# A hybrid decoder layer step: no paged units beside the last head, weight subtractions on GpSimd in two halves, sample rows as sums

## The chip, the cores and the metric

One core of a Trainium2 chip. The metric is the device time of one execution in microseconds (us), the median of several runs. Engines: PE (TensorE matmul; PEld is its weight load), DVE (VectorE), ACT (ScalarE), POOL (GpSimd), SP (SyncE, which issues most of the DMAs).

## What is computed

One layer for a prompt of 1024 rows with 16 meta rows ahead of it, and for 8 sample rows that each have 4096 past positions in a paged cache (32 pages of 128 positions, with keys and values of 512 columns). The model width is 1024, the input projection has 2560 columns, the attention 4 heads with two softmax maps each, the FFN 2816 hidden columns. All is float32.

```
proj = rms_norm(x, ln_mix_pre) @ w_in            # split into q, k, v, a, g
u = a * sigmoid(g)                               # conv group, 512 channels
s = einsum(q, k) * HEAD_DIM**-0.5 - slopes * dist   # causal, two maps per head
p = softmax(s)
o = einsum(p[:, :, 0] - lam * p[:, :, 1], v)
...
attn_out = rms_norm(o, subln) * (1 - lambda_init)
conv_out = silu(layer_norm(causal_depthwise(u, conv_w, conv_b)))
mix = concat([attn_out, conv_out]) @ w_out
x = x + rms_norm(mix, ln_mix_post)
h = rms_norm(x, ln_ffn_pre)
x = x + rms_norm((silu(h @ w_gate) * (h @ w_up)) @ w_down, ln_ffn_post)
```

The sample rows go through the same, with k and v of their own pages ahead of their own row.

## The kernel before

Matmuls of float32 values are made from two parts of each operand: a rounded part H and the rest L = raw - H, so three matmuls stand for one (L149 to L151). A weight row of 128x1024 is brought by `load_split` (L133 to L141): SP loads it as `raw`, ACT casts it to H, and one engine makes L by one subtraction of 128x1024. For 15 rows of `w_in` (wi0 to wi7, wi13 to wi19) and for the 8 rows of `w_out` (wo0 to wo7) this engine is POOL; for the other five of `w_in` it is DVE.

The prompt's rows come in three chunks of columns. `xchunk` (L182 to L204) transposes eight blocks of 128 channels into eight PSUM banks; for each, ACT writes xH, DVE writes xL, and, in the first chunk alone, whose first eight columns are the sample rows, DVE scales these eight columns from PSUM into `xsT`. The sample rows' own projection reads `xsT`.

The stages in time: loads and first chunks (0 to 40 us); the conv group's projections and its depthwise convolution on DVE and POOL (40 to 140 us and on); head by head the projections of q, k, v and the prompt's attention (140 to 442 us, the last head from 372 us on); eight output blocks `c_block` (w_out, residual, norm), of 48 matmuls each; the FFN's gate, up and down to the end.

The prompt's attention of head h runs over eight row blocks i (`attn`, L477 to L575): PE makes the scores in one, two or three pieces (L507), DVE adds the position bias and takes the row's minimum of the negated score (L509), ACT takes the exponentials of both maps (L515), DVE combines them to A = p0 + cc * p1 (L526, in pieces of columns 0 to 400 and the rest, where a row has more than 400), PE transposes A (L534), ACT copies it out (L538), and PE multiplies by the values (L548). After blocks 3 and 7, ACT takes row sums of squares (`junk`, L562), POOL makes their inverse root `or` (L564), ACT scales the head's output `oh` (L566) and PE transposes it (L571).

The samples' paged attention is written as a generator, `dec_units` (L751 to L787). A key unit loads two pages (`page_pair`, by SP, at most 8 page loads ahead), POOL multiplies them by the query (L680, two products of 128x512), and DVE sums the products over 64 columns (L690). With all 16 pairs of a sample done, `dec_max` has DVE make maxima and POOL reduce them over the partitions (L707); `dec_exp` subtracts that maximum on DVE (L712) and takes the exponential on ACT. A value unit loads two value pages and, once for two pairs, issues eight matmuls `pv` on PE (L732). Units are called by `dec_step(rate)`, which adds the rate to what is owed and runs the whole part of it. In the main loop, head h's row blocks call it with `rate_b[h]`, the output blocks with `rate_c`, the FFN's steps with `rate_d`. All of it stands in the order of priorities that a scheduler keeps: a unit's instructions are placed behind the prompt's by an offset, and the scheduler orders the instructions of each engine by its own estimate of when they can start. The flag `kv_n[1]` becomes true once the loop over heads and row blocks is through (L1355).

Of the kernel before, what the change touches and what calls it, by code (L numbers as in the profile page):

```python
# [8 lines left out]
F32 = mybir.dt.float32  # L9
# [3 lines left out]
ALU = mybir.AluOpType  # L13
# [7 lines left out]
DB = 8  # L21
# [25 lines left out]
def tile_layer(ctx: ExitStack, tc: tile.TileContext, I, O, cfg):  # L47
    nc = tc.nc
    V, S, G, T, D = nc.vector, nc.scalar, nc.gpsimd, nc.tensor, nc.sync
# [5 lines left out]
    at = ctx.enter_context(tc.tile_pool(name="at", bufs=cfg["at"]))  # L55
# [4 lines left out]
    def slab(name, dt=F32):  # L60
        return slp.tile([P, SLAB], dt, tag="slab", name=name)

    kv_n = [0, False]
# [66 lines left out]
    def load_raw(src, name, n3=True):  # L130
        raw = slab(name + "r")
        D.dma_start(kn(raw) if n3 else raw[:, :1024], src)
        return raw  # L133

    def load_split(src, name, l_eng, n3=True):
        raw = early.pop(name, None) or load_raw(src, name, n3)
        H = slab(name + "H", F32R)
        S.copy(H[:, :1024], raw[:, :1024])
        L = slab(name + "L", F32R)
        l_eng.tensor_tensor(L[:, :1024], raw[:, :1024], H[:, :1024].bitcast(F32), op=ALU.subtract)  # L140
        return H, L  # L141

    point = {}
# [10 lines left out]
    xH = [slab(f"xH{k}", F32R) for k in range(8)]  # L154
    xL = [slab(f"xL{k}", F32R) for k in range(8)]
# [13 lines left out]
    def xprep(b):  # L169
        rows = DB + META if b < 0 else P  # L170
        xt = x_st.pop(b)
        if "j" not in x_st:
            x_st["j"] = kv("xsq")
        ssq = smt(f"xs{b}", 1)
        S.activation(x_st["j"][:rows], xt[:rows, :DM], AF.Square, accum_out=ssq[:rows])
        r = rstd_of(ssq[:rows], rows, 1.0 / DM, f"xr{b}")
        eng = G if b in cfg["xn_g"] else V
        eng.tensor_scalar(xt[:rows, :DM], xt[:rows, :DM], r[:rows], None, op0=ALU.mult)
        return xt, rows

    xsT = cst.tile([P, 8, DB], F32, name="xsT")
# [3 lines left out]
    def xchunk(c):  # L185
        c0, w = CHUNKS[c]
        blks = [xprep(b) for b in ([-1, 0, 1], [2, 3, 4], [5, 6, 7])[c]]
        if c == 0 and cfg["wi_first"]:
            for ft in (12, 16):
                w_in_load(ft)  # L190
        pts = [f(f"xT{c}{k}") for k, f in enumerate(XPS[c])]
        off = 0
        for xn, rows in blks:
            for k, pt in enumerate(pts):
                T.transpose(out=pt[:, off : off + rows], in_=xn[:rows, k * P : (k + 1) * P], identity=ident[:rows, :rows])
            off += rows
        for k, pt in enumerate(pts):
            wk = wpre[:, k : k + 1]
            S.mul(xH[k][:, c0 : c0 + w], pt[:, :w], wk)
            V.scalar_tensor_tensor(  # L200
                xL[k][:, c0 : c0 + w], pt[:, :w], wk, xH[k][:, c0 : c0 + w].bitcast(F32), op0=ALU.mult, op1=ALU.subtract
            )
            if c == 0:
                V.tensor_scalar(xsT[:, k, :], pt[:, 0:DB], wk, None, op0=ALU.mult)  # L204

    w_in_v = I["w_in"][0].rearrange("(k p) n -> p k n", p=P)

# [6 lines left out]
    def w_in_load(ft):  # L214
        if ft not in ahead:
            ahead[ft] = load_split(w_in_src(ft), f"wi{ft}", V if ft in cfg["wi_v"] else G)
# [454 lines left out]
    def dec_scores(b, st):  # L671
        qB = dec.tile([P, 512], F32, tag="qB", name=f"qB{b}")
        D.dma_start(qB, qsD[b].partition_broadcast(P))
        s = dec.tile([P, NPG + 1, 8], F32, tag="s", name=f"s{b}", bufs=3)
        st[b] = s
        for pg in range(0, NPG, 2):
            kt = page_pair(ck, b, pg, f"k{b}_{pg}")
            n = b * NPG // 2 + pg // 2
            for i in range(2):
                x = G.tensor_tensor(kt[:, i, :], kt[:, i, :], qB, op=ALU.mult)  # L680
            products.append((s[:, pg : pg + 2, :], kt))
            if len(products) > cfg["rlag"]:
                head_sums(x)
            yield b
# [3 lines left out]
    def head_sums(after):  # L688
        s, kt = products.pop(0)
        x = V.tensor_reduce(  # L690
            s.rearrange("p a c -> p (a c)"), kt.rearrange("p a (c d) -> p (a c) d", d=HD), axis=AX.X, op=ALU.add
        )
        if after is not None:
            tc.add_manual_dep(x.ins, after.ins.name, behind, reason="sums behind a later product")

    def dec_max(b, st):
        s = st[b]
        V.tensor_tensor(
            s[:, :NPG, :].rearrange("p g (h j) -> p (g h) j", j=2),
            s[:, :NPG, :].rearrange("p g (h j) -> p (g h) j", j=2),  # L700
            dbias.rearrange("p g h -> p (g h)").unsqueeze(2).to_broadcast([P, NPG * NH, 2]), op=ALU.add,
        )
        V.tensor_copy(s[:, NPG, :], selfs[:, b, :])
        m = smt(f"dm{b}", 8, 2)
        V.tensor_reduce(m, s.rearrange("p g c -> p c g"), axis=AX.X, op=ALU.max)
        mg = smt(f"dg{b}", 8, 2)
        G.partition_all_reduce(mg, m, P, bass.bass_isa.ReduceOp.max)  # L707
        st[b] = s, mg

    def dec_exp(b, st):  # L710
        s, mg = st[b]
        V.tensor_tensor(s, s, mg.unsqueeze(1).to_broadcast([P, NPG + 1, 8]), op=ALU.subtract)  # L712
        S.activation(s, s, AF.Exp)
        st[b] = s
# [5 lines left out]
    def dec_values(b, st):  # L720
        a = st.pop(b)
        pv = pdec(f"pv{b}")
        vs = []
        for pg in range(0, NPG, 2):
            if not vs:
                size = min(cfg["vgrp"] if kv_n[1] else 2, (NPG - pg) // 2)
            vs.append((pg, page_pair(cv, b, pg, f"v{b}_{pg}")))
            if len(vs) == size:
                for q, vt in vs:
                    for i in range(2):  # L730
                        g = (q + i) % 4
                        x = T.matmul(  # L732
                            pv[32 * g : 32 * g + 8, :], lhsT=a[:, q + i, :], rhs=vt[:, i, :],
                            start=q + i < 4, stop=q + i >= NPG - 4, tile_position=(0, 32 * g),
                        )
                        if vt is not vs[-1][1]:
                            tc.add_manual_dep(x.ins, page_dmas[-1], together, reason="pages side by side")
                vs = []
            if pg == NPG // 2:
                dec_total(b, a)  # L740
            yield 0 if vs else size
        pvs = dec.tile([P, 512], F32, tag="gs", name=f"pvs{b}", bufs=2)
        for g in range(4):
            S.copy(pvs[32 * g : 32 * g + 8, :], pv[32 * g : 32 * g + 8, :])
            S.dma_start(pvD[b, g], pvs[32 * g : 32 * g + 8, :])

    def dec_units():
        st = {}
        ks = (b for bb in range(DB) for b in dec_scores(bb, st))
        nk, ready, exped, at = 0, 0, 0, []  # L750
        per = NPG // 2  # L751

        def softmaxes(all_=False):
            nonlocal ready, exped
            while "k" in nat and ready < (nk - len(products)) // per:
                dec_max(ready, st)
                at.append(nk)
                ready += 1
            while exped < ready and (all_ or nk >= at[exped] + cfg["elag"]):
                dec_exp(exped, st)  # L760
                exped += 1

        def keys(n):
            nonlocal nk
            for _ in range(n):
                if nk < DB * per:
                    next(ks)
                    nk += 1
                    if nk == DB * per:
                        while products:  # L770
                            head_sums(None)
                    softmaxes(nk == DB * per)
                    yield

        yield from keys(per + cfg["lag"])
        while "k" not in nat:
            yield "wait"
        softmaxes(True)
        for b in range(DB):
            for n in dec_values(b, st):  # L780
                yield
                yield from keys(n)
# [60 lines left out]
    def w_out_load(k):  # L843
        wo.append(load_split(I["w_out"][0, k * P : (k + 1) * P, :], f"wo{k}", G, n3=False))
# [544 lines left out]
    xn_g=(), wi_first=1, wi_e=(13, 17), sq=0,  # L1389
    behind=-400, w0=7, w1=7, wi_n=1, anchor=1, wi_v=(8, 9, 10, 11, 12), taps=11, conv=400, r2_g=1, hb=5,  # L1390
    vgrp=2, fing=5, ml_g=0, fend=22, cst=0, db=3, cn=6, scn=12, wo0=27, wor=2, c0=7,
    at=8, slabs=35, kv=4, p=6, dve_mul=0, rate_b=(1, 1.25, 1, 0.75), rate_c=1, rate_d=2.45, rate_s=2.2,
    ffn_l=lambda nc: nc.vector,
)
_INS = [
# [39 lines left out]
```

## Time and profile before

| | us |
|---|---|
| median of 3 runs | 1434.7 |
| lowest, highest | 1431.78, 1438.51 |
| the profiled execution | 1440.69 |
| its span in the trace | 1438.8 |
| PE busy | 1357.1 (94%) |
| DVE busy | 860.9 (60%) |
| POOL busy | 595.2 (41%) |
| ACT busy | 551.2 (38%) |
| mean granted clock of PE | 0.977 |

How to read it: the profile shows one execution, 6.0 us longer than the median of the runs. "Busy" is the time in which an engine has an instruction running, and a running instruction may be one that stands still. PE's share is high over the whole span, but the stages differ, and the stage from 372 to 442 us is the one with the least of it.

### The profile page before, as it was taken

The page shows a single profiled execution, that of the slowest core. Times are in us where ns is not written, and L with a number is a line of the kernel's source. Part 1 is how long each engine was busy: PE and PEld are TensorE (multiplying, and loading weights), DVE is VectorE, ACT ScalarE, POOL GpSimd, SP SyncE. Part 2 cuts the span into 40 slices and gives each one's busy share as a digit, 9 for nine tenths or more (in the row PEclk, how much of TensorE's full clock was granted, in tenths as well). Part 3 has the DMA queues.
Part 4 walks back from the last instruction along what each step waited for, and adds up shares of the span by engine and source line. Part 5 has one row for each costly group of instructions (what it writes and reads, how often), then busy time and mean ns, then how long its engine had stood idle before and what let it go on. Part 6 is the DMA issues. An engine that isn't in the chain of part 4 may idle for free.

```text
span 1438.8 us, 21552 instructions
## 1 busy us (share of the span) xinstructions
PE 1357.1 (94%) x6960; PEld 1057.1 (73%) x6960; DVE 860.9 (60%) x1403; ACT 551.2 (38%) x1112; POOL 595.2 (41%) x479
## 2 busy tenths in 40 slices
PE   5999899989869999999999989999999989999997
PEld 5999799979747787777776757676776765666666
DVE  5689996936684567566645465654653374452158
ACT  6566878797764345113021121312121112211122
POOL 4598867445372113745545455464530000000023
PEclk9999999999889999999999999999999999999999
DMA  8211015226535548678867857777677656763454
GB/s 246 86 59 38 27 55 163 75 96 192 170 98 193 171 148 269 211 259 260 262 226 235 265 199 249 235 257 264 204 263 221 214 163 218 229 190 125 147 195 172
DMA packets 199677, 264.34 MB, mean 184 GB/s; under 512 B 16423, under 2 KB 99816, under 8 KB 199557
## 3 DMA queue, kind: packets, MB, share of 16 engines
q1 hardware_dynamic: 188912, 254.40, 54.3%
q10 hardware_dynamic: 10653, 8.57, 1.8%
q8 instruction: 55, 0.90, 0.3%
q14 instruction: 57, 0.47, 0.1%
HBM read 245.92 MB, written 17.48 MB: 183 GB/s over the span
## 4 chain that ended last, share of the span: by engine, by line
PE 59%; SPq 3%; DMA 3%; issue 3%; DVE 3%; POOL 2%; ACT 1%; POOLq 0%; DVEq 0%; ACTq 0%
PE dn L149 5%; PE pu L149 5%; PE dn L150 5%; PE dn L151 5%; PE pu L151 5%; PE pu L150 5%; PE pg L149 5%; PE pg L150 5%; PE pg L151 5%; PE pv L732 4%; PE mo L151 2%; PE mo L149 2%; PE mo L150 2%; DMA v<-in_cache_v 2%; SPq L665 2%
## 5 line engine op out<-in xcount | busy, mean ns | idle before, releaser
L680 POOL TENSOR_TENSOR k<-k,qB 128x512 f32<-128x512 f32 x256 | 353.5, 1409 | 230.2 <-DMA k<-in_cache_k 176.3
L690 DVE TENSOR_REDUCE s<-k 128x16 f32<-128x1024 f32 x128 | 154.8, 1213 | 101.1 <-POOL k L680 100.9
L956 ACT CAST wH<-wr 128x1024 fp32r<-128x1024 f32 x66 | 69.0, 1048 | 239.4 <-DVE wL L958 124.6
L149 PE MATMUL dn<-wH,aH 128*128 128x512 f32 x352 | 141.3, 405 | 5.0 <-DVE y L999 3.4
L149 PE MATMUL pu<-hH,wH 128*128 128x512 f32 x352 | 141.2, 401 | 1.1 <-DVE y L999 1.1
L150 PE MATMUL dn<-wL,aH 128*128 128x512 f32 x352 | 140.9, 400 | 0.0
L151 PE MATMUL pu<-hH,wL 128*128 128x512 f32 x352 | 139.2, 396 | 1.6 <-DVE wL L958 1.6
L151 PE MATMUL dn<-wH,aL 128*128 128x512 f32 x352 | 140.7, 400 | 0.0
L149 PE MATMUL pg<-hH,wH 128*128 128x512 f32 x352 | 140.4, 399 | 0.0
L150 PE MATMUL pu<-hL,wH 128*128 128x512 f32 x352 | 140.1, 398 | 0.0
L150 PE MATMUL pg<-hL,wH 128*128 128x512 f32 x352 | 139.3, 396 | 0.0
L151 PE MATMUL pg<-hH,wL 128*128 128x512 f32 x352 | 139.2, 395 | 0.0
L958 DVE TENSOR_TENSOR wL<-wr,wH 128x1024 fp32r<-128x1024 f32 x66 | 93.7, 1420 | 46.3 <-ACT wH L956 22.2
L999 DVE TENSOR_TENSOR y<-dn,y 128x512 f32<-128x512 f32 x144 | 95.5, 684 | 38.0 <-PE dn L151 37.1
L414 POOL TENSOR_TENSOR cb<-cb 128x512 f32<-128x512 f32 x80 | 102.9, 1316 | 18.0 <-ACT cb L413 9.9
L1071 POOL TENSOR_TENSOR y<-y,wfpost 128x512 f32<-128x512 f32 x10 | 17.6, 1772 | 206.7 <-ACT ft L1069 206.6
L423 DVE SCALAR_TENSOR_TENSOR acc<-u,cw,acc 128x512 f32<-128x512 f32 x144 | 98.7, 747 | 0.2
L982 ACT CAST aH<-sg 128x512 fp32r<-128x512 f32 x44 | 27.3, 620 | 167.6 <-DVE sg L975 167.5
L149 PEld LDWEIGHTS dn<-wH,aH 128*128 128x128 f32 x352 | 67.5, 192 | 31.8 <-DVE y L999 6.8
L149 PEld LDWEIGHTS pu<-hH,wH 128*128 128x128 f32 x352 | 66.4, 189 | 29.4 <-issue 12.9
L975 DVE TENSOR_TENSOR sg<-sg,pu 128x512 f32<-128x512 f32 x44 | 30.1, 683 | 94.0 <-PE pu L151 94.0
L149 PEld LDWEIGHTS pg<-hH,wH 128*128 128x128 f32 x352 | 66.1, 188 | 27.4 <-issue 11.6
(581 smaller groups left out, 2969.5 us busy)
## 6 DMA issues: line engine op xcount, KB each, us to landing
k<-in_cache_k SPq DMA_DIRECT2D x256, 256.0 KB
v<-in_cache_v SPq DMA_DIRECT2D x256, 256.0 KB
wr<-in_w_gate SPq DMA_DIRECT2D x22, 512.0 KB
wr<-in_w_up SPq DMA_DIRECT2D x22, 512.0 KB
wr<-in_w_down SPq DMA_DIRECT2D x22, 512.0 KB
sd<-in_w_down SPq DMA_DIRECT2D x22, 512.0 KB
sw_gate<-in_w_gate SPq DMA_DIRECT2D x20, 512.0 KB
sw_up<-in_w_up SPq DMA_DIRECT2D x20, 512.0 KB
```

Of the source, the lines that this page charges most:

```text
L149: T.matmul(out, lhsT=wH, rhs=xH, start=first, stop=False)
L150: T.matmul(out, lhsT=wH, rhs=xL, start=False, stop=False)
L151: mark(T.matmul(out, lhsT=wL, rhs=xH, start=False, stop=last))
L414: G.tensor_tensor(accp, accp, t, op=ALU.add)
L423: V.scalar_tensor_tensor(dst, src, cw[:, ct, k : k + 1], acc, op0=ALU.mult, op1=ALU.add)
L680: x = G.tensor_tensor(kt[:, i, :], kt[:, i, :], qB, op=ALU.mult)
L690: x = V.tensor_reduce(s.rearrange("p a c -> p (a c)"), kt.rearrange("p a (c d) -> p (a c) d", d=HD), axis=AX.X, op=ALU.add)
L732: x = T.matmul(pv[32 * g : 32 * g + 8, :], lhsT=a[:, q + i, :], rhs=vt[:, i, :], start=q + i < 4, stop=q + i >= NPG - 4, tile_position=(0, ...
L956: S.copy(H[:, :1024], raw[:, :1024])
L958: V.tensor_tensor(L[:, :1024], raw[:, :1024], H[:, :1024].bitcast(F32), op=ALU.subtract)
L975: V.tensor_tensor(sg, sg, o, op=ALU.mult)
L999: V.tensor_tensor(y[b][:, ws], o, y[b][:, ws], op=ALU.add)
```

## The change

Four edits. `load_split` splits POOL's subtraction into two of 128x512; DVE's stay whole. `xsT` is no longer scaled from PSUM inside the loop over the eight banks, but is the sum xH + xL of the same eight columns, from SBUF, in a loop behind. The exponential of a sample's scores is allowed only once `kv_n[1]` is set, or in a call with `all_`. The rate of paged units beside head 3 goes from 0.75 to 0, and that beside the output blocks from 1 to 1.75.

```diff
         S.copy(H[:, :1024], raw[:, :1024])
         L = slab(name + "L", F32R)
-        l_eng.tensor_tensor(L[:, :1024], raw[:, :1024], H[:, :1024].bitcast(F32), op=ALU.subtract)
+        for a in (0, 512) if l_eng is G else (0,):
+            e = a + 512 if l_eng is G else 1024
+            l_eng.tensor_tensor(L[:, a:e], raw[:, a:e], H[:, a:e].bitcast(F32), op=ALU.subtract)
         return H, L
...
-            if c == 0:
-                V.tensor_scalar(xsT[:, k, :], pt[:, 0:DB], wk, None, op0=ALU.mult)
+        if c == 0:
+            for k in range(8):
+                V.tensor_tensor(xsT[:, k, :], xH[k][:, 0:DB].bitcast(F32), xL[k][:, 0:DB].bitcast(F32), op=ALU.add)
...
-            while exped < ready and (all_ or nk >= at[exped] + cfg["elag"]):
+            while exped < ready and (all_ or kv_n[1] and nk >= at[exped] + cfg["elag"]):
                 dec_exp(exped, st)
                 exped += 1
...
-    at=8, slabs=35, kv=4, p=6, dve_mul=0, rate_b=(1, 1.25, 1, 0.75), rate_c=1, rate_d=2.45, rate_s=2.2,
+    at=8, slabs=35, kv=4, p=6, dve_mul=0, rate_b=(1, 1.25, 1, 0), rate_c=1.75, rate_d=2.45, rate_s=2.2,
```

What POOL has in its order beside head 3, from wo2 on, before (wo2L to wo7L are the subtractions of `w_out`, k_12 to k_16 the products of key pages, `or` the root of a head's row sums):

```order
L140 TENSOR_TENSOR wo2L<-wo2r,wo2H 128x1024
L680 TENSOR_TENSOR k_12_4847<-k_12_4847,qB_4070 128x512
L140 TENSOR_TENSOR wo3L<-wo3r,wo3H 128x1024
L564 TENSOR_TENSOR or_4841<-ssq_3954,mhalf 128x4
L140 TENSOR_TENSOR wo4L<-wo4r,wo4H 128x1024
L140 TENSOR_TENSOR wo5L<-wo5r,wo5H 128x1024
L680 TENSOR_TENSOR k_14_5090<-k_14_5090,qB_4070 128x512 x2
L140 TENSOR_TENSOR wo6L<-wo6r,wo6H 128x1024
L680 TENSOR_TENSOR k_16_5242<-k_16_5242,qB_4070 128x512
L140 TENSOR_TENSOR wo7L<-wo7r,wo7H 128x1024
L564 TENSOR_TENSOR or_5072<-ssq_4874,mhalf 128x4
```

and after, at the same place:

```order
L142 TENSOR_TENSOR wo2L<-wo2r,wo2H 128x512 x2
L683 TENSOR_TENSOR k_12_4862<-k_12_4862,qB_4084 128x512
L142 TENSOR_TENSOR wo3L<-wo3r,wo3H 128x512 x2
L567 TENSOR_TENSOR or_4856<-ssq_3968,mhalf 128x4
L142 TENSOR_TENSOR wo4L<-wo4r,wo4H 128x512 x2
L142 TENSOR_TENSOR wo5L<-wo5r,wo5H 128x512 x2
L142 TENSOR_TENSOR wo6L<-wo6r,wo6H 128x512 x2
L142 TENSOR_TENSOR wo7L<-wo7r,wo7H 128x512 x2
L567 TENSOR_TENSOR or_5034<-ssq_4889,mhalf 128x4
```

The products of pairs 14 and 16 have left this place for the output blocks; the product of pair 12 and the roots kept theirs, and each subtraction is now two in a row.

DVE's order around the first paged exponential's subtraction (s minus dg), amid the scores and combinations of head 3, before:

```order
L526 SCALAR_TENSOR_TENSOR p_4772<-p_4785,cc_4800,p_4772 128x640
L509 ISA p_4908,nm_4902<-S_0_4909,alibi 128x272
L509 ISA nm_4902 128x1
L526 SCALAR_TENSOR_TENSOR p_4876<-p_4881,cc_4888,p_4876 128x144
L712 TENSOR_TENSOR s_2014<-s_2014,dg_4769 128x264
L509 ISA p_4965,nm_4964<-S_0_4966,alibi 128x400
```

and after:

```order
L529 SCALAR_TENSOR_TENSOR p_4787<-p_4800,cc_4815,p_4787 128x640
L512 ISA p_4923,nm_4917<-S_0_4924,alibi 128x272
L512 ISA nm_4917 128x1
L529 SCALAR_TENSOR_TENSOR p_4891<-p_4896,cc_4903,p_4891 128x144
L715 TENSOR_TENSOR s_2024<-s_2024,dg_4784 128x264
L512 ISA p_4954,nm_4953<-S_0_4955,alibi 128x400
```

Nothing moved here: the subtraction stands in the same row of DVE's order in both.

DVE's order in the first chunk of `xchunk`, the first two of the eight banks, before:

```order
L200 SCALAR_TENSOR_TENSOR xL_102<-xT_192,wpre,xH_94 128x280
L204 TENSOR_SCALAR xsT<-xT_192,wpre 128x8
L123 TENSOR_SCALAR xr_t<-xs_262 128x1
L178 TENSOR_SCALAR xt_148<-xt_148,xr_r 128x1024
L200 SCALAR_TENSOR_TENSOR xL_103<-xT_193,wpre,xH_95 128x280
L204 TENSOR_SCALAR xsT<-xT_193,wpre 128x8
```

and after:

```order
L202 SCALAR_TENSOR_TENSOR xL_102<-xT_193,wpre,xH_94 128x280
L207 TENSOR_TENSOR xsT<-xH_94,xL_102 128x8
L123 TENSOR_SCALAR xr_t<-xs_263 128x1
L202 SCALAR_TENSOR_TENSOR xL_103<-xT_194,wpre,xH_95 128x280
L180 TENSOR_SCALAR xt_148<-xt_148,xr_r 128x1024
L207 TENSOR_TENSOR xsT<-xH_95,xL_103 128x8
```

The scheduler still puts each sample sum close behind its xL, and the second xL now stands ahead of the row block's normalization `xt`.

## Rows read from the trace of the kernel before

**Rows 1.** Three stages: stretch, length, busy PE PEld DVE ACT POOL, PEclk, DMA share, GB/s.

```profile
140.00:215.00 75.00, 66.75 (x405) 63.61 (x404) 72.93 (x151) 62.19 (x141) 56.59 (x44) 0.95 0.14 41
...
372.00:442.00 70.00, 46.41 (x268) 39.69 (x267) 49.97 (x124) 44.88 (x117) 35.40 (x22) 0.78 0.47 149
442.00:700.00 258.00, 257.46 (x1202) 194.38 (x1202) 155.41 (x215) 81.10 (x165) 106.05 (x87) 1.00 0.68 221
```

**Rows 2.** PE's waits, 372 to 442 us: in total, times, longest (us).

```profile
PE S L507 <- DVE nm L509: 11.1, 6, 4.1
PE oT L571 <- ACT oh L566: 4.8, 1, 4.8
```

**Rows 3.** DVE's timeline beside head 3: start, duration, operation [idle before, releaser].

```profile
390.61 0.43 DVE L712 TENSOR_TENSOR s<-s,dg 128x264 f32<-128x264 f32 x1 [4.55 <-POOL dg L707]
...
402.27 1.22 DVE L690 TENSOR_REDUCE s<-k 128x16 f32<-128x1024 f32 x1 [4.85 <-POOL k L680]
...
403.82 2.39 DVE L526 SCALAR_TENSOR_TENSOR p<-p,cc,p 128x400 f32<-128x400 f32 x1
...
407.92 2.44 DVE L526 SCALAR_TENSOR_TENSOR p<-p,cc,p 128x400 f32<-128x400 f32 x2
...
411.78 2.42 DVE L526 SCALAR_TENSOR_TENSOR p<-p,cc,p 128x400 f32<-128x400 f32 x2
...
416.06 1.16 DVE L526 SCALAR_TENSOR_TENSOR p<-p,cc,p 128x400 f32<-128x400 f32 x2
...
422.07 3.08 DVE L526 SCALAR_TENSOR_TENSOR p<-p,cc,p 128x400 f32<-128x400 f32 x2
...
425.57 4.63 DVE L526 SCALAR_TENSOR_TENSOR p<-p,cc,p 128x400 f32<-128x400 f32 x2
```

**Rows 4.** DVE's timeline in earlier heads, L526 issued while POOL ran nothing.

```profile
227.29 1.43 DVE L526 SCALAR_TENSOR_TENSOR p<-p,cc,p 128x400 f32<-128x400 f32 x2
...
251.42 0.63 DVE L526 SCALAR_TENSOR_TENSOR p<-p,cc,p 128x400 f32<-128x400 f32 x1
```

**Rows 5.** POOL's timeline beside head 3.

```profile
390.18 0.39 POOL L707 PARTITION_ALL_REDUCE dg<-dm  x1 [8.26 <-issue]
...
399.76 3.70 POOL L680 TENSOR_TENSOR k<-k,qB 128x512 f32<-128x512 f32 x3
403.43 2.34 POOL L140 TENSOR_TENSOR wo2L<-wo2r,wo2H 128x1024 fp32r<-128x1024 f32 x1
405.74 1.60 POOL L680 TENSOR_TENSOR k<-k,qB 128x512 f32<-128x512 f32 x1
...
429.48 2.92 POOL L140 TENSOR_TENSOR wo7L<-wo7r,wo7H 128x1024 fp32r<-128x1024 f32 x1
432.37 1.01 POOL L564 TENSOR_TENSOR or<-ssq,mhalf 128x4 f32<-128x4 f32 x1
```

**Rows 6.** ACT's timeline, the cast of the last `w_out` row.

```profile
428.34 1.03 ACT L138 CAST wo7H<-wo7r 128x1024 fp32r<-128x1024 f32 x1
```

**Rows 7.** PE's timeline, the value matmuls beside head 3.

```profile
423.25 1.04 PE L732 MATMUL pv<-v,s 128*8 128x512 f32 x8
```

**Rows 8.** DVE's and POOL's timelines, the combination of block 0 (144 columns), head 0 and head 3.

```profile
168.48 2.41 DVE L526 SCALAR_TENSOR_TENSOR p<-p,cc,p 128x144 f32<-128x144 f32 x1
...
168.32 2.41 POOL L140 TENSOR_TENSOR wi1L<-wi1r,wi1H 128x1024 fp32r<-128x1024 f32 x1
...
385.71 0.35 DVE L526 SCALAR_TENSOR_TENSOR p<-p,cc,p 128x144 f32<-128x144 f32 x1
```

**Rows 9.** DVE's and POOL's timelines at the first chunk; where `xsT` is read.

```profile
28.40 0.22 DVE L204 TENSOR_SCALAR xsT<-xT,wpre 128x8 f32<-128x8 f32 x1
...
29.01 2.40 POOL L140 TENSOR_TENSOR wi13L<-wi13r,wi13H 128x1024 fp32r<-128x1024 f32 x1 [1.75 <-ACT wi13H L138]
...
L623 PE MATMUL sq<-swq,xsT x16: 592/592/597, 63.1 to 64.4; 128*8 128x512 f32 x16
```

**Rows 10.** PE's waits from 600 us to the end: in total, times, longest (us).

```profile
PE pv L732 <- DMA v<-in_cache_v: 10.9, 6, 6.8
```

## The prediction

> **What bounds the kernel now.** I read the table of stages first [rows 1]. From 442 us on PE is the limit: 257.46 of 258 us are busy at a granted clock of 1.00. Whatever the change takes from VectorE or GpSimd there is worth nothing, and whatever it adds to PE counts in full. Two stages are different. In 140 to 215 us DVE is the limit (72.93 of 75 us), and in 372 to 442 us, the attention of head 3, no engine is: PE has 46.41 of 70 us, DVE 49.97, POOL 35.40, and the clock is 0.78, the lowest of all stages. Most of the change lies there, so I read that stretch next, wait by wait and then engine by engine.
>
> PE's waits there [rows 2] are 11.1 us for row maxima and scores that DVE makes (L509), and one wait of 4.8 us for the scaled head output. Both lead back to one pattern between DVE and POOL. The combination of the two softmax maps, L526, reads two SBUF tiles. Undisturbed, its first piece of 400 columns takes 0.63 us, both pieces of a full row block take 1.43 us, and in row block 5 they take 1.16 [rows 3, 4]; that is 0.13 us for each block of 128 columns, so blocks 2 to 7 want 0.63, 0.90, 1.03, 1.16, 1.30 and 1.43 us. Block 2's was issued at 403.82 and took 2.39 us: it ended at 406.21, 0.44 us after POOL's subtraction wo2L, which ran from 403.43 to 405.77; POOL's next product then took 1.60 us, where three in a row take 3.70 [rows 3, 5]. So the two engines shut each other out, an instruction at a time. The other five took 2.44, 2.42, 1.16, 3.08 and 4.63 us [rows 3]. Waits of 1.76, 1.54, 1.39, 0, 1.78 and 3.20 us are **9.7 us** in all.
>
> Behind the last of these the chain goes through POOL once more: wo7L takes 2.92 us from 429.48, because ACT's cast of that weight row only starts at 428.34 [rows 5, 6]; the root of the row sums (L564) stands behind it in POOL's order, runs at 432.37, and PE's wait of 4.8 us ends after that. There is a second knot at 390 us: POOL's all-reduce runs after 8.26 us in which POOL does nothing the profile shows, DVE stands 4.55 us at the first paged exponential's subtraction (L712), and later 4.85 us for the key products that POOL begins at 399.76 [rows 3, 5].
>
> **The exponential's gate.** In the order of instructions nothing is moved by it: the first exponential is reached through the call with all_ true, which the new condition lets pass, and later ones come after the flag is set. L712 stands in the same row of DVE's queue in both kernels, amid head 3's scores. So the 4.55 us and the 8.26 us stay: 0 us.
>
> **The rates.** 0.75 beside each of eight row blocks is 6 paged units, with 8 more in the output blocks: 14. Now it is none, and 1.75 in each of eight blocks: 14. The FFN starts at the same unit. What leaves head 3 on POOL are the products of two page pairs (four of 128x512); on DVE two key sums leave the end of the stage; on SP the page loads stand behind the loads of wo4 to wo7, the two norm weights and the first mixed rows, which now wait for nothing. Products 10 and 12 stay where they were, so the waits of 4.85 us stay. One set of eight value matmuls, 1.04 us at 423.25 [rows 7], moves out of PE's idle time into the stage where PE has no idle time: **+1.0 us**. In 442 to 700 us POOL is busy for 106 of 258 us [rows 1], so six more units' products lie beside PE's work, at nothing; if that cover goes, the price is a wait for pages (rival C).
>
> **The halved subtractions.** POOL's work is the same, in pieces of half of 2.34 us [rows 5], 1.2 us each, an estimate that takes a fixed cost of nothing; the upper bound on a fixed cost is what two products of the same 128x512 shape take beyond one 128x1024 subtraction, 2 x 1.23 - 2.34 = 0.1 us. What it changes is how long DVE is shut out. I laid POOL's new order along DVE's old times. Block 2 meets the rest of one half (0.8 us). Block 3's two pieces meet both halves of wo3L (1.9). Blocks 4 and 5 meet ends of halves (0.2 and 0.6). Block 6 meets none, because the products of pair 14, which ran beside it, are gone. Block 7 meets about one half (1.45). That leaves 5.0 of 9.7 us: 4.7 gained. Against it, a DVE operation now gets in between the halves of wo0L, so the all-reduce comes some 0.7 us later. **-4.0 us** in all, and the end of the stage follows: the last exponential, wo7's cast and wo7L move with it, and the root behind wo7L is the next thing that PE waits for, as before. Bounds: -9.7 (no wait is left) to +0.7 (the halves only alternate with DVE's pieces, and the all-reduce is late).
>
> In the DVE-bound stage one L526 of 144 columns took 2.41 us behind wi1L (168.32, 2.41 us), where 0.35 is its own time [rows 8]; behind a half it would wait about 1.2 us less: **-1.2 us** (0 to -2.0).
>
> **The sample rows.** Eight scalings of 128x8 from PSUM [rows 9], 0.13 us from one start to the next, become eight adds of two SBUF tiles, behind all eight of xL. A PSUM bank is released by xL, 0.13 us earlier. Against it the adds can be shut out as L526 was: they stand in the stretch of wi13L (29.01, 2.40 us) [rows 9]. I take 0, since the prompt's matmuls need xH and xL alone, and the sample rows are first used at 63.1 us [rows 9]; -1.0 (eight times 0.13) to +2.5 (one subtraction of two halves) are the ends. The Trainium skill, "SBUF — State Buffer", in "Who interferes with whom", says that a VectorE instruction with two SBUF inputs contends with a GpSimd instruction that reads SBUF, while one with at most one SBUF input outside the 2-port modes doesn't; this speaks against the edit, since it turns the second kind into the first. By it the sum would lie up to the upper end above, and L526 at 403.82 agrees with it.
>
> Heads 0 to 2 are also interleaved a little differently, with the same instructions. DVE and PE there have no single large wait; I take 0, with 3 us either way (one more subtraction of 2.4 us shut out, or one less).
>
> **Sum.** -4.0 - 1.2 + 1.0 = -4.2 us. The profiled execution took 1440.7 us (span 1438.8), so it would take 1436.5. That execution is 6.0 us above the median of 1434.7, which I take off again: **1430.5 us**.
>
> **Rivals.** A: no lock wait is left. With fewer products and halves that never meet a pair of pieces, -9.7 - 2.0 - 1.0 + 1.0 = -11.7, so 1423.0. For it: the four products of pairs 14 and 16 ran right beside blocks 6 and 7, which hold 5.0 of the 9.7 us. Against it: wo2L to wo5L are still queued back to back beside blocks 2 to 5. B: the change doesn't do what it says. The gate moves nothing, the halves alternate with DVE's pieces so that each piece waits for a half and the pair for a whole, and only the value matmuls and the later all-reduce are left: +1.0 + 0.7, 1436.4. For it: POOL's 1.60 us product shows that the waiting engine goes first at a hand-over, but only for one instruction. C, slower: the output blocks become page-bound. Their 14 units need 28 page loads on SP in order, between the loads of mixed rows, and PE stops at the value matmuls as it does in the FFN, where it lost 10.9 us in six waits, the longest 6.8 [rows 10]. The same again, on the forecast, is 1430.5 + 10.9 = 1441.4, and on B 1447. It decides once a page arrives later than the block that issues its matmuls, that is, if the DMA share in 442 to 700 us (0.68 [rows 1]) has no room for six more units in eight blocks. Against it: those blocks' own weights are loaded already, and PE lost 0.54 us there so far.
>
> **Chances and range.** Forecast 0.45 (1427 to 1434), A 0.24, B 0.14, C 0.17. From the low end of A with 3 us of heads 0 to 2 (1420) to C at 1441 and a little over, which leaves some 0.1 at each end: **1420 to 1442**. A measurement of this kernel can tell about 0.5%, 7.2 us, from no change: faster than 1427.5 is A and the lower edge of the forecast, 0.35; slower than 1441.9 is half of C and a little of B, 0.12; 0.53 lies within.
>
> **What would show it.** In the profile after: L526 rows of blocks 2 to 7 of head 3 summing to about 11.4 us instead of 16.1; the stage ending about 4 us earlier; POOL's all-reduce still behind some 8 us of nothing and L712 still waiting; a value set of eight matmuls more in the FFN; the PE wait for pages near 10.9 us. A wait for pages in the output blocks speaks for C; L526 at its undisturbed times for A. The forecast is wrong if the new interleaving in 0 to 372 us moves the start of head 3 by more than 3 us, which no row here can exclude.

## The result and the profile after

The changed kernel takes 1445.99 us (median of 15 runs, 1440.43 to 1454.7), the kernel before 1436.75 us (15 runs, 1431.78 to 1448.5). The ratio is **1.0055**, with a 95% interval of 1.0031 to 1.0080: slower by some 8 us (by the medians 9.2), outside the range of the prediction, and on the other side. The difference is small, but the interval leaves no change out. The profiled execution has a span of 1445.7 us, 6.9 above that of before.

The table of stages after (stretch, length, busy PE PEld DVE ACT POOL, clock, DMA share, GB/s), beside [rows 1]; the first row is before's:

```profile
215.00:372.00 157.00, 150.75 (x1043) 146.22 (x1042) 98.64 (x242) 134.75 (x340) 83.94 (x73) 0.98 0.41 131
...
215.00:372.00 157.00, 147.20 (x1010) 142.36 (x1010) 95.83 (x239) 132.92 (x336) 80.04 (x73) 0.98 0.40 128
372.00:442.00 70.00, 46.92 (x264) 40.91 (x263) 42.21 (x122) 46.70 (x121) 32.50 (x28) 0.78 0.34 112
442.00:700.00 258.00, 253.41 (x1190) 190.16 (x1192) 153.81 (x211) 80.91 (x166) 104.15 (x87) 1.00 0.67 223
```

From 215 to 372 us PE is busy 3.6 us less. Beside head 3 DVE has 7.8 us less to do, and PE's time is about the same. From 442 to 700 us PE stands for 4.6 us, where it stood for 0.5.

To see where the time went I set each matmul of a trace against the matmul of the same name in before, and took the median shift of 20 us of them (positive is later). The columns show it from 120, 360, 440, 560 and 1400 us of before on:

| kernel | 120 | 360 | 440 | 560 | 1400 | ratio (95%) |
|---|---|---|---|---|---|---|
| the change | -3.3 | +2.2 | +2.3 | +5.0 | +7.0 | 1.0055 (1.0031 to 1.0080) |
| halves | -2.3 | +7.9 | +8.7 | +8.4 | +9.8 | 1.0069 (1.0041 to 1.0096) |
| sums | +2.6 | +9.6 | +6.3 | +6.0 | +3.9 | 1.0040 (1.0021 to 1.0059) |
| halves_sums | -1.8 | +3.3 | +1.3 | +1.3 | +5.0 | 1.0029 (1.0007 to 1.0051) |
| halves_win | +1.3 | +9.9 | +7.9 | +7.6 | +6.3 | 1.0080 (1.0053 to 1.0108) |
| half_one_row | -1.6 | +9.0 | +5.7 | +5.8 | +8.2 | 1.0051 (1.0026 to 1.0077) |
| halves_wout | +0.6 | +0.6 | -1.9 | -1.9 | +1.5 | 0.9995 (0.9969 to 1.0020) |
| halves_same_order | -0.9 | -1.2 | -4.8 | -4.8 | -2.4 | 0.9972 (0.9949 to 0.9995) |
| rates | +0.9 | +1.0 | +1.9 | +4.5 | +3.8 | 1.0038 (1.0020 to 1.0057) |
| rate_b_only | -2.1 | -2.1 | -3.0 | -3.4 | +5.8 | 1.0119 (1.0084 to 1.0155) |
| rates_loads_held | -2.4 | -1.8 | -1.9 | +0.7 | +0.5 | 1.0011 (0.9992 to 1.0029) |
| reduce_behind | -1.8 | -0.6 | -11.0 | -5.6 | -4.8 | 0.9908 (0.9876 to 0.9939) |
| reduce_behind_wo | -2.6 | -1.1 | -11.2 | -6.4 | -8.2 | 0.9962 (0.9945 to 0.9978) |
| reduce_behind_six | -4.0 | -1.7 | -14.0 | -9.5 | -17.3 | 0.9939 (0.9915 to 0.9963) |
| after_reduce_behind | -0.7 | +5.7 | -6.7 | -2.7 | -2.9 | 0.9994 (0.9979 to 1.0010) |

A column is one execution, so it scatters: five kernels (halves_wout, halves_same_order, rates, rate_b_only and rates_loads_held) keep the order of before on ACT, DVE and PE until head 3, and they stand at -2.4 to +0.9 at 120 us. The 3.3 us that the change seems to gain by then are hardly beyond that. From 120 to 360 us these five move by -0.3 to +0.6 us only, so the next differences are larger than the scatter: 5.5 us lost between 120 and 360 us, nothing gained in head 3 (360 to 440), 2.7 us lost in the output blocks (440 to 560). Another 2.0 us by 1400 us are not traced to a place. halves_sums has the order of the change on ACT, DVE and PE until 423 us; it loses 5.0 us from 120 to 360 us, and then gains 2.0 us in head 3.

**The stretch to 360 us.** PE's longest new wait there, from PE's waits of 215 to 372 us after (in total, times, longest), and its row:

```profile
PE o L551 <- ACT metaT L541: 5.0, 2, 4.9
...
312.94 0.79 PE L551 MATMUL o<-vm,metaT 128*128 128x128 f32 x2 [4.85 <-ACT metaT L541]
```

Before, PE stood at the same place for 3.01 us, ahead of the scores of the next row block. That row of PE, then ACT's timeline before and, below it, after:

```profile
310.24 0.59 PE L507 MATMUL S<-R,L 128*128 128x272 f32 x1 [3.01 <-ACT vT L277]
...
309.43 0.40 ACT L515 ACTIVATE p<-p,nm 128x144 f32<-128x144 f32 x1
...
309.83 0.36 ACT L277 COPY vT<-pv 128x272 f32<-128x272 f32 x1
310.21 1.28 ACT L1155 ACT_TABLE_LOAD   x1
311.50 1.25 ACT L1155 ACTIVATE mTs<-mTs,clnb,clnw 128x8 f32<-128x8 f32 x4
312.66 0.24 ACT L538 COPY metaT<-AT 16x128 f32<-16x128 f32 x1
...
310.20 1.28 ACT L1158 ACT_TABLE_LOAD   x1
311.50 1.24 ACT L1158 ACTIVATE mTs<-mTs,clnb,clnw 128x8 f32<-128x8 f32 x4
312.65 0.24 ACT L541 COPY metaT<-AT 16x128 f32<-16x128 f32 x1
...
313.17 0.37 ACT L280 COPY vT<-pv 128x272 f32<-128x272 f32 x1
```

Before, the copy of vT out of PSUM stands ahead of a table load (ACT_TABLE_LOAD, 1.28 us) and four activations of the samples, and PE's next scores start at 310.24. After, the copy stands behind them, at 313.17, and in PE's order two value matmuls (o) now stand ahead of those scores. They need metaT, which ACT copies at 312.65, behind the table load and the activations as before, so PE's wait lasts until 312.94. This place costs 4.85 - 3.01 = 1.8 of the 5.5 us; the shift grows by another 2.4 us between 180 and 220 us, and the rest is spread. None of the four edits names these instructions; the scheduler put them in another order.

**Head 3.** DVE's L526 (L529 after) meets shorter pieces, as forecast. Blocks 2 to 7, beside [rows 3]:

```profile
408.48 1.31 DVE L529 SCALAR_TENSOR_TENSOR p<-p,cc,p 128x400 f32<-128x400 f32 x1
...
411.51 2.37 DVE L529 SCALAR_TENSOR_TENSOR p<-p,cc,p 128x400 f32<-128x400 f32 x2
...
415.29 1.03 DVE L529 SCALAR_TENSOR_TENSOR p<-p,cc,p 128x400 f32<-128x400 f32 x2
...
418.17 1.47 DVE L529 SCALAR_TENSOR_TENSOR p<-p,cc,p 128x400 f32<-128x400 f32 x2
...
424.31 1.30 DVE L529 SCALAR_TENSOR_TENSOR p<-p,cc,p 128x400 f32<-128x400 f32 x2
...
427.93 2.03 DVE L529 SCALAR_TENSOR_TENSOR p<-p,cc,p 128x400 f32<-128x400 f32 x2
```

That is 9.5 us where it was 16.1: 6.6 us of waits are gone. But the all-reduce ahead of them came later. POOL and DVE after, beside [rows 3, 5]:

```profile
394.73 0.39 POOL L710 PARTITION_ALL_REDUCE dg<-dm  x1 [10.54 <-issue]
...
395.16 0.43 DVE L715 TENSOR_TENSOR s<-s,dg 128x264 f32<-128x264 f32 x1 [6.83 <-POOL dg L710]
```

POOL stood 10.54 us ahead of it instead of 8.26, and DVE 6.83 instead of 4.55. Behind that, the stage ran 3.6 us faster from L715 to PE's first oT (39.7 us, 43.3 before), and gave 1.5 of that back by the first mo (9.8 us, 8.3 before).

### The profile page after: what moved, and what is told of

Same layout as the page of the kernel before. It is cut to its first block, busy times and chain, and to the rows that moved or that the text cites. A ratio compares the mean times of both kernels' runs of the same rounds, so it can differ in the third digit from the quotient of the medians.

```text
span 1445.7 us, 21569 instructions
## 1 busy us (share of the span) xinstructions
PE 1358.7 (94%) x6960; PEld 1058.2 (73%) x6960; DVE 856.1 (59%) x1403; ACT 552.1 (38%) x1112; POOL 596.5 (41%) x502
## 4 chain that ended last, share of the span: by engine, by line
PE 54%; DMA 4%; issue 4%; DVE 4%; SPq 3%; POOL 2%; ACT 1%; POOLq 0%; DVEq 0%; ACTq 0%
PE dn L151 5%; PE dn L152 5%; PE dn L153 5%; PE pu L151 5%; PE pu L153 5%; PE pu L152 5%; PE pg L152 4%; PE pg L151 4%; PE pg L153 4%; PE pv L735 3%; DMA v<-in_cache_v 2%; PE mo L151 2%; PE mo L152 2%; PE mo L153 2%; SPq L668 2%
## 5 line engine op out<-in xcount | busy, mean ns | idle before, releaser
L426 DVE SCALAR_TENSOR_TENSOR acc<-u,cw,acc 128x512 f32<-128x512 f32 x144 | 98.8, 747 | 0.2
```

The lines of the kernel that those rows point to most:

```text
L426: V.scalar_tensor_tensor(dst, src, cw[:, ct, k : k + 1], acc, op0=ALU.mult, op1=ALU.add)
```

## The experiments

Every ratio is against the kernel before on the same chip. Theory P: two places lose, the order of instructions in heads 0 to 2 (by the halves) and the output blocks (by the rates). Theory N: no place loses much, and the trace's differences are chance. The gate has no run of its own: halves_sums, which lacks it, has the order of the change until 423 us.

**The parts alone.** Each hunk of the change as it stands in the diff above; halves_sums has the halves and the sums.

halves: 

> POOL's subtractions halved, nothing else changed. Theory P (two places lose): the halves put the instructions of heads 0 to 2 in another order, in which ACT's copy of vT (L280) comes behind a table load and PE waits near 310 us; against before the trace should lose some 3 to 5 us between 200 and 320 us and nothing in the FFN: ratio 1.002 to 1.004. Theory N (chance of single traces, and the all-reduce's preparation): ratio within 0.002 of 1. The forecast's term (lock waits shortened) would give 0.996 to 0.998.

sums: 

> Sample rows as sums alone. Theory P: the first chunk's normalisations come earlier on DVE, PE is some 3 us ahead at 40 us (in the changed kernel 3.3 us); what is left at the end depends on the order of heads 0 to 2 that this start gives: ratio 0.998, or 1.000 if it is lost there. Theory N: ratio within 0.002 of 1, and PE at 40 us within 1 us.

rates: 

> Rates 0 beside head 3 and 1.75 beside the output blocks, alone. Theory P: 3 to 5 us lost between 442 and 740 us, where the changed kernel's PE had 4.6 us idle in 442 to 700 instead of 0.5 (page waits 2.8, weights 1.0, mixed rows 0.7) and one more set of value matmuls, against 2 to 4 us gained beside head 3 with the products gone: ratio 1.000 to 1.002. Theory N: within 0.002 of 1. The forecast: 0.998 to 0.999.

halves_sums: 

> Halves and sums together, the rates as before. Theory P: start 3 us ahead, heads 0 to 2 lose 5 us (the same order at 310 us as in the whole change), FFN as before: ratio 1.001 to 1.003, so the whole change's 1.0055 less what the rates cost. Theory N: within 0.002 of 1.

Measured 1.0069, 1.0040, 1.0038 and 1.0029. No part is a gain, which speaks against N and against the forecast. Halves and sums cost together less than the 1.0109 that their prices add up to (the interval ends at 1.0051): what they cost is not a price for each piece. P had the sign for halves and rates, but both cost more than it said. It missed for the sums alone, which lose 7.0 us between 120 and 360 us, with an order of their own.

**Which halves.**

```diff
# halves_wout
-        for a in (0, 512) if l_eng is G else (0,):
-            e = a + 512 if l_eng is G else 1024
+        for a in (0, 512) if name[:2] == "wo" else (0,):
+            e = a + 512 if name[:2] == "wo" else 1024
# halves_win: if l_eng is G and name[:2] == "wi"
# halves_same_order: if name[:2] == "wo" or name in ("wi13", "wi17", "wi18", "wi19", "wi3", "wi7")
# half_one_row: if name == "wi16"
```

halves_wout: 

> Only the eight rows of w_out are subtracted in halves; the order of ACT, DVE and PE is that of before in every row, POOL's differs only in those pieces. Theory P: the loss of 'halves' comes from the order of heads 0 to 2, so it is gone here, and what is left is the gain that the forecast wanted beside head 3, some 2.5 to 4 us: ratio 0.997 to 0.999. Rival (the halves themselves cost, by a fixed cost per instruction or by hand-overs between DVE and POOL): ratio 1.002 or more.

halves_win: 

> Only the fifteen rows of w_in that POOL subtracts are halved. Theory P: PE loses 5 us near 205 us and 2 to 3 us near 310 us as with all halves, and head 3 gains nothing: ratio 1.005 to 1.008. Rival: less than 1.002.

halves_same_order: 

> Fourteen of the 23 rows halved: wi13, 17, 18, 19, 3, 7 and all of w_out, chosen because with them every engine's order is that of before, row by row. Theory P (the order costs, not the halves): ratio 0.997 to 1.002. Rival (the halves cost by themselves): 14/23 of the 0.7% of all halves, 1.004.

half_one_row: 

> One row halved, wi16, the first; the order of ACT then differs from row 20 on and that of PE from row 58 on. Theory P: PE loses some 3 to 8 us in 140 to 372 us, nothing later: ratio 1.002 to 1.007. Rival (the halves cost by themselves): 1/23 of 0.7%, 1.000.

Measured 0.9995, 1.0080, 0.9972 and 1.0051; halves_wout lies a little above what P said, the others within it. This separates the pieces from their order. Fourteen halved rows that leave every other engine's order alone cost nothing (a gain, if a small one); one halved row that changes the order from the start on costs 0.5%. In the table, the five kernels of the same order move by -0.3 to +0.6 us between 120 and 360 us; seven kernels of other orders (the change, halves, sums, halves_sums, halves_win, half_one_row and after_reduce_behind) by +5.0 to +10.6. The three other kernels with reduce_behind in their names have yet another order, from 10 us on, and move by +1.1 to +2.2. So another order can also cost little; which one it is decides.

What the other order does in half_one_row can be read off one place, where the shift grows by 8.9 us (from the matmuls of 180 to 200 us to those of 200 to 220). PE's and DVE's timelines there, then the stretches 205 to 215 us of before and, below the dots, of half_one_row:

```profile
208.98 0.55 PE L510 MATMUL S<-R,L 128*128 128x456 f32 x1 [3.78 <-DVE u L426]
...
208.18 0.74 DVE L426 SCALAR_TENSOR_TENSOR u<-u,cw,acc 128x512 f32<-128x512 f32 x1
...
205.00:210.00 5.00, 5.00 (x29) 4.80 (x29) 4.84 (x13) 2.48 (x6) 0.00 (x0) 1.00 0.00 0
210.00:215.00 5.00, 5.00 (x39) 4.97 (x38) 4.84 (x16) 4.76 (x12) 0.87 (x1) 1.00 0.42 129
...
205.00:210.00 5.00, 1.12 (x3) 0.30 (x2) 4.91 (x14) 1.39 (x4) 0.00 (x0) 0.92 0.34 105
210.00:215.00 5.00, 3.48 (x15) 3.08 (x16) 4.87 (x14) 3.35 (x9) 0.20 (x1) 0.50 0.00 0
```

DVE is busy in both. In half_one_row its last taps of the convolution (L426) come later, among the row minima of these scores, at 208.18 where before has the first of them at 202.78 (L423), and PE's next scores start only when this one has ended. PE stands 3.78 us with projection matmuls queued behind, and the clock granted after that is 0.50 of full speed (1.2 of 2.4 GHz) from 210 to 215 us, so the 15 matmuls there take longer too.

**The rates and the all-reduce.**

```diff
# rate_b_only: only rate_b of the rates
-rate_b=(1, 1.25, 1, 0.75)
+rate_b=(1, 1.25, 1, 0)
# rates_loads_held: both rates, and in load_raw and dec_max
+        if name in ("wo4", "wo5", "wo6", "wo7"):
+            tc.add_manual_dep(x.ins, point["ar"], together, reason="behind the code change")
...
+        point.setdefault("ar", x.ins.name)
# reduce_behind: both rates, and in softmaxes and dec_max ("root" is set at L564 of head 3's block 7)
-            while "k" in nat and ready < (nk - len(products)) // per:
+            while "root" in point and "k" in nat and ready < (nk - len(products)) // per:
...
+        if b == 0:
+            tc.add_manual_dep(x.ins, point["root"], behind, reason="behind the last head")
```

rate_b_only: 

> Rate 0 beside head 3, and 1, as before, beside the output blocks; six units go to the FFN. Theory P: the 3 us that the changed rates lose between 500 and 560 us come from 1.75 units a block (page loads late for their matmuls), so they are not lost here; but the all-reduce's preparation is as late as with both rates (POOL idle some 11 us before it, as SP's w_out loads stand unbroken beside it), and six units' value matmuls lie in the FFN: ratio 1.000 to 1.002. Rival (the loss is the page traffic in the FFN, whatever the rate): 1.003 or more.

rates_loads_held: 

> Both new rates; every engine's order as in 'rates', but the load of wo4 (and so, in SP's order, those of wo5 to wo7) waits for the first all-reduce. Theory P: POOL's preparation of the all-reduce is long with these rates (11.5 us idle, 8.3 before) because four loads of 0.5 MB are issued right beside it; held, it takes 6 to 7 us, and head 3 ends 3 to 5 us earlier than with the rates alone: ratio 0.999 to 1.001 against 1.0038. Rival (chance of a trace): the idle time stays at 8 us or more, ratio 1.003 to 1.005.

reduce_behind: 

> Both new rates, whole subtractions, and the first sample's maxima, all-reduce and exponential really behind head 3's attention: POOL's all-reduce stands after the last root in its order. Theory P: the 7.8 us that DVE waits for it beside head 3 with these rates (4.6 before) are gone, so 4 to 8 us of the stage; the output blocks lose up to 3 us to late pages as in 'rates': ratio 0.996 to 0.999, against 1.0038 for the rates alone. Rival (the wait only moves: PE waits for the late exponential, or POOL's roots of the output blocks stand behind the code change): 1.001 or more.

Measured 1.0119, 1.0011 and 0.9908. POOL's all-reduce in rates, rate_b_only, rates_loads_held and reduce_behind:

```profile
394.31 0.39 POOL L710 PARTITION_ALL_REDUCE dg<-dm  x1 [11.47 <-issue]
...
389.73 0.40 POOL L707 PARTITION_ALL_REDUCE dg<-dm  x1 [9.89 <-DMA wo7r<-in_w_out]
...
386.47 0.39 POOL L712 PARTITION_ALL_REDUCE dg<-dm  x1 [6.39 <-PE AT L539]
...
442.76 0.39 POOL L712 PARTITION_ALL_REDUCE dg<-dm  x1 [5.96 <-issue]
```

SP's issues at that time, before and, below the dots, in rates:

```profile
382.17 0.86 SPq L665 DMA_DIRECT2D v<-in_cache_v  x2
384.30 0.34 SPq L132 DMA_DIRECT2D wo4r<-in_w_out  x1
384.73 0.38 SPq L132 DMA_DIRECT2D wo5r<-in_w_out  x1
385.21 0.38 SPq L132 DMA_DIRECT2D wo6r<-in_w_out  x1
...
382.92 0.34 SPq L132 DMA_DIRECT2D wo4r<-in_w_out  x1
383.35 0.38 SPq L132 DMA_DIRECT2D wo5r<-in_w_out  x1
383.82 0.38 SPq L132 DMA_DIRECT2D wo6r<-in_w_out  x1
384.30 0.63 SPq L132 DMA_DIRECT2D wo7r<-in_w_out  x1
```

Ahead of each all-reduce POOL's sequencer runs two instructions that reconfigure POOL. What before has of them, for its eight all-reduces (times in ns, first and last start in us):

```profile
L707 POOLq MODIFY_POOL_CONFIG  x16: 1/11/21, 381.9 to 1067.1; - x16
```

The first start when wo0L ends, and then POOL stands, though the maxima that it reduces are ready 4.7 to 10.0 us ahead of it (58 to 61 where it runs behind head 3). With four loads of 0.5 MB in one run beside it (the three kernels with rate 0 beside head 3, the all-reduce in it and nothing held) POOL stands 9.9 to 11.5 us; with pages between them, 6.1 to 8.3 (before, the halves' kernels, half_one_row, halves_sums); with the loads held, 6.4; with the loads out 4 us earlier, 5.9 (sums); behind head 3, in a quiet stretch, 5.6 to 6.0 (the four kernels with reduce_behind in their names). rates and rates_loads_held have the same order on ACT, DVE and PE, so there it is the loads. How a load delays it is not shown, and each figure is of one execution; the other all-reduces of these kernels, in the FFN, stand 5.8 to 9.9 us. The Trainium skill, "GPSIMD Engine Reference", "2.1 Instruction dispatch", has about 6 us for the first call to a freshly loaded kernel, with no instruction seen in the profile; the quiet case agrees (5.96 us in reduce_behind), and the others show it as a floor, since beside loads it was up to 5.5 us longer. What the hold is worth is less sure: 1.0011 stands against 1.0038, but their intervals overlap, and in the traces it is 1.0 us of head 3 and nothing more behind it.

rate_b_only missed P's ratio by far: its output blocks lose nothing (-3.0 to -3.4 us in the table), as P had it, but the six units end up in the FFN, where PE waits on DVE's sums of the down projection, 19.8 us in three waits (2.4 in one in the change, 3.4 in two before).

reduce_behind gained more than P said. It does for the first sample's all-reduce and exponential what the gate did not: both run behind head 3 (the maxima are still made in it, 60 us earlier). PE then gains 10.4 us from 360 to 440 us, and the 5.4 us that are lost again by 560 us (PE's first mo waits 1.4 us for mH, two waits of 0.5 to 0.9 for the first FFN weights, and value matmuls in a stage that PE fills) leave a gain. Its trace is that of its slowest run (1435.43 us, median 1426.32), so the column at 1400 us shows less than the ratio. Its order also differs from that of rates from 10 us on; in the trace this costs 1.1 us between 120 and 360 us (0.1 in rates).

**Together.**

```diff
# after_reduce_behind: the whole change, and the edit of reduce_behind
# reduce_behind_wo: reduce_behind, and the halves of halves_wout
# reduce_behind_six: reduce_behind, and halves of wi13, wi17, wi18, wi19, wi3, wi7 only
```

reduce_behind_wo: 

> The version with the all-reduce behind the last head, and the rows of w_out in halves. If the forecast's term beside head 3 holds without the knot of the all-reduce, 2 to 4 us less than 0.9908: ratio 0.988 to 0.990. If the halves only alternate with DVE's pieces, or the last weights bound the stage by ACT's casts: 0.991, as without them.

after_reduce_behind: 

> The whole change, and the first sample's maxima, all-reduce and exponential really behind head 3's attention. If the late all-reduce of the rates (POOL idle 10.5 us, DVE waiting 6.8) is what the change lacks beside head 3, 1.0055 falls by what 'reduce_behind' has less than 'rates' (1.0038 - 0.9908 = 0.0130): ratio 0.991 to 0.996. The cost of the order in heads 0 to 2 stays. Rival (that gain was chance, or page waits in the FFN take it back): 0.999 or more.

reduce_behind_six: 

> 'reduce_behind' with six rows of w_in halved that leave every engine's order as it is there (wi13, 17, 18, 19, 3, 7). If halves alone cost nothing and 'reduce_behind' was measured rightly: 0.989 to 0.993. If 0.9908 was chance and its true value is that of 'reduce_behind_wo': 0.995 to 0.997.

Measured 0.9962, 0.9994 and 0.9939; none of the three lies where it was expected. With the whole change the edit gains 0.6%, half of what was expected, and the ratio is in the range of the rival (0.999 or more). In the traces head 3 gains 12.4 us from 360 to 440 (10.1 to 12.2 in the three others with this edit), so the gain of the stage is no chance; 4.0 are lost by 560, while heads 0 to 2 lose 6.4 (5.5 in the change without it). What the rest was is open: the orders differ behind head 3 too. The order of reduce_behind is that of reduce_behind_six, which gives 0.9939, on another chip, so its size is 0.6 to 0.9%. The halves of w_out don't add to it: 0.9962 is worse, with an interval that lies above that of 0.9908. They reorder ACT, DVE and PE from 427 us on; their term is no longer there to be gained, or lost again by that, which the runs don't tell apart. **reduce_behind beats both kernels**, the one before by 0.9% (0.6 to 1.2), in six runs.

## Why the prediction was wrong

*The interleaving of heads 0 to 2* ("I take 0, with 3 us either way") is the step that failed first. It was bounded by the price of one subtraction, as if the order could only move one wait. Its reason, that PE has "no single large wait" there, was a misreading: PE waits 3.01 us for vT at 310.24 before, the place that got worse. The scheduler works out the order from its own times of every instruction, so halved pieces at 20 us change what stands next to what at 205 and 310 us, and PE, which is busy for 150.75 of the 157 us from 215 to 372 us in before, has little to gain there and much to lose. It cost 5.5 us in the trace. The prediction had named a move of head 3's start by more than 3 us as its sign of being wrong; the matmuls at 360 us come 2.2 us later than before, 5.5 later than those at 120 us let expect. half_one_row and halves_same_order show that it is the order. The order itself was at hand, and ACT's vT behind the table load could have been read from it.

*The all-reduce* ("So the 4.55 us and the 8.26 us stay: 0 us", and 0.7 us for the halves of wo0L) is the second. That the gate moves nothing was right. But the prediction saw that w_out's loads "now wait for nothing" and did not ask what they would run into: POOL's 8.26 us of idle time [rows 5] was taken as a constant, and it became 10.54. DVE's wait behind it grew by the same 2.3 us, against a term of -4.0. What that is worth at the stage's end is open: halves_sums, with the old rates and 6.93 us, gains 2.0 us in head 3 and the change nothing, but rates_loads_held, with 5.1 us less of POOL's idle time than rates, ends head 3 only 1.0 us earlier.

*The lock waits* were right in mechanism. 6.6 us of 9.7 are gone (4.7 forecast). What was mis-sized is what this is worth at the stage's end: halves_wout takes 3.95 us from L529's waits (12.18 us where 16.13 were) and ends head 3 2.5 us earlier; its ratio can't be told from 1. halves_same_order, with the same order, ends it 3.6 us earlier, at 0.9972. So where the order stays the term of -4.0 is not far off; in the change nothing of it is left at the stage's end. Where the waits end, ACT takes over: after, the last exponential starts only at 426.14, behind the cast of wo6 at 425.05 and a piece of L512 that stands behind block 6's combination.

*L526 of 144 columns* beside wi1L took 2.41 us [rows 8] and takes 1.44 after, close to the 1.2 us less that were forecast, but by luck. DVE's row and POOL's after:

```profile
164.97 1.44 DVE L529 SCALAR_TENSOR_TENSOR p<-p,cc,p 128x144 f32<-128x144 f32 x1
...
164.95 1.29 POOL L417 TENSOR_TENSOR cb<-cb 128x512 f32<-128x512 f32 x1 [0.28 <-ACT cb L416]
166.20 2.61 POOL L142 TENSOR_TENSOR wi1L<-wi1r,wi1H 128x512 fp32r<-128x512 f32 x2
```

It now stands beside a product of the convolution and ends at 166.41, 0.2 us behind the start of wi1L's halves (166.20): that is the other order, not the half.

*The output blocks* (+1.0 for one value set) were right in sign, and short of the 2.7 us that were lost. In the trace 0.7 of it is a wait of the first mo for `oh`, 1.0 the first FFN weights; the same growth is in rates and rates_loads_held (2.6), so it is the rates' own.

*The sample rows* (0, -1.0 to +2.5): most adds take 0.15 us, three met a subtraction and took 0.8. What they cost by themselves wasn't isolated, since sums alone has another order, too. *Rival C* (pages) didn't come: PE's waits for pages are 12.2 us from 442 us on, 10.9 before, and none of them is in the output blocks (442 to 560). *Rival B* named the sign, but not the places; C on B, 1447, lies near the measured time by luck.

## What to carry to other kernels

Where a scheduler orders the instructions, a change of one instruction's length can be a change of the order everywhere behind it, and a new dependency even ahead of it (reduce_behind's order differs from 10 us on, though its edit is beside head 3). Compare the orders of both kernels first, look for what PE waits for (a PSUM copy behind a table load, taps of a convolution among the row minima), and try the edit on the instructions that leave the order alone; what is left is the edit's own price. And when work leaves a stage, ask what moves up in its place: here loads that slowed the one step for which everything waited.

## What was not expected of the hardware

POOL's preparation of an all-reduce isn't a constant: 5.6 to 6.0 us in a quiet stretch, 6.1 to 8.3 beside page and weight loads, 9.9 to 11.5 beside four loads of 0.5 MB in a row. The way back may behave likewise: with the loads held behind the all-reduce, POOL's next operation came 9.4 us after it started (386.47 to 395.85), where it was 7.5 us in rates (394.31 to 401.77) with the loads over by then. That is one execution; in the other kernels it was 7.1 to 8.2 us behind the first all-reduce, 7.4 to 7.8 in a quiet stretch.
